# Layer 0's attention in groups of four heads, with mask and sink on VectorE and PE's order fixed in the source

## The chip, the cores and the metric

The kernel runs on one core of a Trainium2 chip. A core has five engines that work side by side, each through its own queue in order: TensorE (PE, with its weight loads shown apart as PEld), VectorE (DVE), ScalarE (ACT), GpSimd (POOL) and SyncE (SP), which here issues transfers. PE writes its results into PSUM, eight banks of 512 f32 columns by 128 partitions; the other data is in SBUF. The metric is the device time of one execution in microseconds (us).

## The reference

A model of several layers of mixed kinds runs on 512 latent positions and 256 context positions of width 1024, all in f32. The change lies in the first layer's mixer, windowed attention with grouped keys and a sink: 16 query heads of 64 columns, 4 key and value heads, each used by 4 query heads. Latent queries are taken in 4 blocks of 128; a block sees itself, its neighbours and all context keys, and within the neighbours only keys at most 128 positions away. Context queries see the context alone.

```python
def softmax_with_sink(s, sink):
    sk = sink.astype(jnp.float32)[None, :, :, None, None]
    m = jnp.maximum(jnp.max(s, axis=-1, keepdims=True), sk)
    e = jnp.exp(s - m)
    return e / (jnp.sum(e, axis=-1, keepdims=True) + jnp.exp(sk - m))
...
        s_lat = jnp.einsum('bqhgd,bkhd->bhgqk', q, k).astype(jnp.float32)
        s_lat = jnp.where(ok, s_lat, NEG_INF)
        s_ctx = jnp.einsum('bqhgd,bkhd->bhgqk', q, k_ctx).astype(jnp.float32)
        p = softmax_with_sink(jnp.concatenate([s_lat, s_ctx], axis=-1), sink_g).astype(v.dtype)
        return (jnp.einsum('bhgqk,bkhd->bqhgd', p[..., :n_loc], v)
                + jnp.einsum('bhgqk,bkhd->bqhgd', p[..., n_loc:], v_ctx))
```

## The kernel before

The program runs the whole model in one launch: layer 0 (this attention and an MLP), layer 1 (a gated scan and an MLP), then a second block (attention with relative positions, a state-space layer, a mixture of experts). Only `layer0_attn` and a helper that it calls are touched.

By the time attention begins, queries `Q` (one tile per head), keys split into a high and a low part (`KH`, `KL`, one each per key head) and values `V` are in SBUF. There are six query blocks `qb` of 128 rows: 0 and 1 are context, 2 to 5 latent. For one query block and one query head (called a head here; there are 6 x 16 = 96) the kernel does the following.

- Scores, in `scores`: matmuls of Q with KH and KL for the latent keys (L618, L619; 384 columns where a block has two neighbours, 256 where it has one), a matmul of the identity with a bf16 mask for each neighbour (L621, L623), matmuls with KH and KL for the 256 context keys (L624, L625), and one of a single column for the sink (L626). So qb 3 and 4 have five key tiles of 128 (640 columns), qb 2 and 5 four, and qb 0 and 1 the two of the context. All of it lands in a two-bank PSUM tile, of which there are two.
- Softmax: DVE takes the negated maximum of a row (L627), ACT the exponential with its sum (L635), from PSUM into `p`, DVE the reciprocal of the sum (L637), and POOL multiplies (L638). The score banks come free when the exponential has read them.
- Values, in `values`, for two key heads (eight heads) at a time and one key tile per step: twice four transposes of p on PE into one bank (L659), copied to SBUF as `pt` by ACT and by DVE (L662), and a pair of value matmuls of 512 columns, one into the upper and one into the lower 64 rows of a bank (L666), which `K.together` keeps side by side. After the last key tile DVE copies the result out (L674).

The loop runs over twelve blocks of eight heads. Between the heads of one block it emits the value steps of the block before. In six places it also runs `K.mod_half`, half of a modulation vector: 32 matmuls of 256 columns with weights loaded into the `raw` buffers (L362), a copy by ACT, and four transposes (L369). After the loop the first two units of the output projection's weights w_o are made ready by `K.unit`: a load into `raw`, a cast on ACT (L221) and a subtraction on DVE (L222). `K.mod_affine` follows, with transposes for a gate (L428). The order of PE's instructions is chosen by the scheduler of the tile framework from the order of emission and from dependences; the other engines' too.

The tiles `p` lie in a pool of ten, and three of a block's in the `wlo` weight buffers; `pt` lies in the `whi` weight buffers and in a tile of its own.

Of the kernel before, what the change touches and what calls it, by code (L numbers as in the profile page):

```python
# [19 lines left out]
P = 128  # L20
# [130 lines left out]
class Kern:  # L151
# [196 lines left out]
    def mod_half(self, pool, l, m, half, tag="rows", raws=("raw", "raw"), own=None):  # L348

        nc = self.nc  # L350
# [14 lines left out]
        rows = pool.tile([P, 4, P], F32, tag=tag, name=self.nm("rows"), bufs=1)  # L365
        nc.scalar.copy(rows, b.rearrange("p (k t) -> p k t", k=4))
        b = self.bank()
        for k in range(4):
            nc.tensor.transpose(b[:, k * P:k * P + P], rows[:, k], self.ident)  # L369
        c0 = 8 * m + 4 * half  # L370
        v = b.rearrange("p (k s r) -> p k r s", k=4, s=4)[:, :, 0:2, :]
        nc.vector.tensor_reduce(self.modT[l][:, c0:c0 + 4, :], v, axis=AX.X, op=ALU.add)  # L372
        bm = self.sm(f"b_mod{l}")[:, c0:c0 + 4]
        nc.vector.tensor_add(self.modT[l][:, c0:c0 + 4, :], self.modT[l][:, c0:c0 + 4, :],
                             bm[:, :, None].to_broadcast([P, 4, 2]))
# [138 lines left out]
def layer0_attn(K):  # L514
# [11 lines left out]
    with ExitStack() as left:  # L526
# [5 lines left out]
        mask = qp.tile([P, 2, P], BF, name="mask")  # L532
        nc.gpsimd.memset(mask, 0.0)
        nc.gpsimd.affine_select(mask[:, 0], mask[:, 0], pattern=[[1, P]], compare_op=ALU.is_ge, fill=NEG,
                                base=0, channel_multiplier=-1)
        nc.gpsimd.affine_select(mask[:, 1], mask[:, 1], pattern=[[-1, P]], compare_op=ALU.is_ge, fill=NEG,
                                base=0, channel_multiplier=1)

        sk = qp.tile([P, 3, 16], BF, name="sk")
        sr = qp.tile([P, 16], F32, name="sr")  # L540
        sink3 = qp.tile([P, 16], BF, name="sink3")
        one3 = qp.tile([P, P], BF, name="one3")
        nc.vector.memset(sink3, 0.0)
        nc.vector.memset(one3, 0.0)
        nc.vector.memset(one3[0:3], 1.0)
        nc.vector.tensor_copy(sk[:, 0], K.sm("sink"))
        nc.vector.tensor_sub(sr, K.sm("sink"), sk[:, 0])
        nc.vector.tensor_copy(sk[:, 1], sr)
        nc.vector.tensor_sub(sr, sr, sk[:, 1])
        nc.vector.tensor_copy(sk[:, 2], sr)  # L550
        for k in range(3):
            nc.scalar.dma_start(sink3[k:k + 1], sk[0:1, k])
# [45 lines left out]
        with K.right("att", 2) as ap:  # L598
            def scores(qb, j):

                lat = qb >= 2
                bl = qb - 2
                w0, w1 = (max(bl - 1, 0), min(bl + 1, 3)) if lat else (0, -1)
                nl = (w1 - w0 + 1) * P
                a0 = 512 - nl
                n = nl + NCTX + 1
                qs = slice(qb * P, qb * P + P)
                nmx, den = K.tiny(4), K.tiny(4)
                pr = []
                if lat and j % 2 == 0:  # L610
                    three = K.w.tile([P, 2048], F32, tag="wlo", name=K.nm("p3"))[:, :1926]
                    three = three.rearrange("p (g n) -> p g n", g=3)
                for g in range(4):
                    h = 4 * j + g
                    S = K.bank2()
                    if lat:
                        ks = slice(NCTX + w0 * P, NCTX + w0 * P + nl)
                        nc.tensor.matmul(S[:, a0:512], Q[h][:, qs], KH[j][:, ks], start=True, stop=False)  # L618
                        nc.tensor.matmul(S[:, a0:512], Q[h][:, qs], KL[j][:, ks], start=False, stop=False)  # L619
                        if w0 < bl:  # L620
                            nc.tensor.matmul(S[:, a0:a0 + P], K.identb, mask[:, 0], start=False, stop=w1 == bl)  # L621
                        if w1 > bl:
                            nc.tensor.matmul(S[:, 512 - P:512], K.identb, mask[:, 1], start=False, stop=True)  # L623
# [1498 lines left out]
```

## Time and profile before

Three runs took 2281.13, 2284.09 and 2289.94 us; the median is 2284.09.

| | us |
|---|---|
| profiled execution, its own time | 2287.39 |
| its span, first to last instruction | 2285.7 |
| PE busy | 2147.8 (94%) |
| PE weight loads busy | 1773.3 (78%) |
| DVE busy | 1391.3 (61%) |
| ACT busy | 963.6 (42%) |
| POOL busy | 321.6 (14%) |
| layer 0's attention, first score matmul to first output projection | 193.4 (142.0 to 335.4) |
| mean granted PE clock of the execution | 0.974 |

The busy times are those of the whole span; engines overlap, so they don't add up to it. The ends of matmuls are modelled and overlap the next ones, so that the distance between the starts of two instructions tells more of what PE spends than the durations do. "Granted clock" is the share of PE's full clock (2.4 GHz) that the chip allowed; 0.5 is its other level (1.2 GHz), and a value between them is a mean over a stretch.

### The profile page before, as it was taken

How to read it: one execution, taken by the hardware profiler on the slowest of the kernel's cores; microseconds unless marked ns; L12 is line 12 of the kernel's file. 1: busy time of each engine (PE TensorE's matmuls, PEld its weight loads, DVE VectorE, ACT ScalarE, POOL GpSimd, SP SyncE). 2: the span in 40 equal slices, each digit the busy share in tenths (PEclk: the TensorE clock that was granted, in tenths of full speed). 3: DMA queues.
4: the chain of work that ended last, by engine and by line, in shares of the span. 5: the costliest groups of instructions: out<-in, count | busy, mean ns of one | idle time of the engine just before them, and what ended most of it. 6: DMA issues, size and time to landing. Idle time of an engine off the chain costs nothing. (4 is left out here: it accounts for less than half of the span.)

```text
span 2285.7 us, 30405 instructions
## 1 busy us (share of the span) xinstructions
PE 2147.8 (94%) x12104; PEld 1773.3 (78%) x12104; DVE 1391.3 (61%) x2343; ACT 963.6 (42%) x1504; POOL 321.6 (14%) x357
## 2 busy tenths in 40 slices
PE   6999989999999999999989999999899997998986
PEld 5876658888888888789977887888799874776864
DVE  4665664899745444641794598555646764547974
ACT  5445555521221221542554532322353453536864
POOL 0025432112000000410000100000220000013422
PEclk9999999999999999999999999999999998998998
DMA  7123021457411211111211224232322435468992
GB/s 289 65 102 112 37 87 44 175 188 254 157 56 56 74 64 66 56 53 56 94 38 38 87 89 151 96 112 81 122 93 93 152 125 125 179 241 289 318 296 73
DMA packets 58064, 279.09 MB, mean 122 GB/s; under 512 B 9345, under 2 KB 13841, under 8 KB 33089
## 3 DMA queue, kind: packets, MB, share of 16 engines
q1 hardware_dynamic: 38048, 219.39, 27.3%
q0 software_dynamic: 18768, 55.04, 7.6%
q10 hardware_dynamic: 1104, 2.70, 0.3%
q8 instruction: 96, 1.57, 0.3%
q14 instruction: 48, 0.39, 0.1%
HBM read 264.54 MB, written 24.08 MB: 126 GB/s over the span
## 5 line engine op out<-in xcount | busy, mean ns | idle before, releaser
L221 ACT CAST whi<-raw 128x2048 fp32r<-128x2048 f32 x106 | 202.4, 1910 | 561.6 <-PE b L252 390.0
L222 DVE TENSOR_TENSOR wlo<-raw,whi 128x2048 fp32r<-128x2048 f32 x106 | 245.1, 2314 | 224.5 <-ACT whi L221 224.3
L250 PE MATMUL b<-hl,whi 128*128 128x512 f32 (+1 forms) x736 | 284.0, 386 | 2.5 <-DVE t L323 1.5
L248 PE MATMUL b<-hl,whi 128*128 128x512 f32 (+1 forms) x736 | 283.0, 385 | 0.8 <-ACT whi L221 0.8
L252 PE MATMUL b<-hl,wlo 128*128 128x512 f32 (+1 forms) x736 | 281.7, 386 | 0.0
L823 DVE TENSOR_TENSOR acc<-acc,b 128x512 f32<-128x512 f32 x280 | 180.8, 682 | 157.0 <-PE b L252 156.7
L248 PE MATMUL b<-whi,hid 128*128 128x512 f32 x640 | 215.5, 395 | 2.6 <-ACT whi L221 1.9
L250 PE MATMUL b<-wlo,hid 128*128 128x512 f32 x640 | 216.7, 394 | 0.0
L252 PE MATMUL b<-whi,hid 128*128 128x512 f32 x640 | 215.0, 395 | 0.0
L250 PEld LDWEIGHTS b<-hl,whi 128*128 128x128 f32 x736 | 139.1, 189 | 30.6 <-issue 3.1
L248 PEld LDWEIGHTS b<-hl,whi 128*128 128x128 f32 x736 | 139.0, 189 | 30.1 <-ACT whi L221 1.3
L252 PEld LDWEIGHTS b<-hl,wlo 128*128 128x128 f32 x736 | 139.3, 189 | 28.3 <-issue 0.2
L1978 DVE TENSOR_TENSOR wlo<-raw,whi 128x2048 fp32r<-128x2048 f32 x57 | 129.9, 2287 | 32.4 <-ACT whi L1978 32.4
L252 PEld LDWEIGHTS b<-whi,hid 128*128 128x128 f32 x640 | 120.3, 188 | 27.9
L248 PEld LDWEIGHTS b<-whi,hid 128*128 128x128 f32 x640 | 119.2, 188 | 29.2 <-ACT whi L221 2.1
L250 PEld LDWEIGHTS b<-wlo,hid 128*128 128x128 f32 x640 | 120.4, 188 | 27.5
L638 POOL TENSOR_TENSOR p<-p,t 128x512 f32<-128x512 f32 (+2 forms) x96 | 91.6, 969 | 177.8 <-DVE modT L372 90.3
L1978 ACT CAST whi<-raw 128x2048 fp32r<-128x2048 f32 x57 | 108.3, 1912 | 10.4 <-PE b L242 10.4
L395 DVE CUSTOM_DVE_ANT_0 junk<-mw,cb 128x1024 bf16<-128x1024 f32 x80 | 97.5, 1219 | 3.2 <-DMA mw<-in_w_modT_dram 2.6
L240 PE MATMUL b<-whi,hl 128*128 128x256 f32 x320 | 91.3, 285 | 2.3 <-ACT qr L1486 2.3
L241 PE MATMUL b<-wlo,hl 128*128 128x256 f32 x320 | 91.5, 286 | 0.0
L242 PE MATMUL b<-whi,hl 128*128 128x256 f32 x320 | 91.1, 285 | 0.0
(617 smaller groups left out, 4736.9 us busy)
## 6 DMA issues: line engine op xcount, KB each, us to landing
raw<-in_w_e_dram SPq DMA_DIRECT2D x57, 1024.0 KB, 7.2
raw<-in_w_mlp_in_dram SPq DMA_DIRECT2D x32, 1024.0 KB, 4.8
raw<-in_w_mlp_out_dram SPq DMA_DIRECT2D x32, 1024.0 KB, 4.8
mw<-in_w_modT_dram POOLq DMA_DIRECT2D x56, 512.0 KB, 4.5
raw<-in_w_mod_dram SPq DMA_DIRECT2D x20, 1024.0 KB, 7.7
raw<-in_w_in_dram SPq DMA_DIRECT2D x16, 1024.0 KB, 4.7
raw<-in_gla_in_dram SPq DMA_DIRECT2D x12, 1024.0 KB, 4.7
raw<-in_w_o_dram SPq DMA_DIRECT2D x8, 1024.0 KB, 4.7
```

Source lines behind the costliest of these rows:

```text
L221: ins = self.nc.scalar.copy(hi, r).ins
L222: ins = ins, (self.nc.gpsimd if pool else self.nc.vector).tensor_sub(lo, r, hi.bitcast(F32)).ins
L240: mm(out, ah, bh, start=start, stop=False)
L241: mm(out, ah, bl, start=False, stop=False)
L242: mm(out, al, bh, start=False, stop=stop)
L248: mm(o, ah, b, start=start, stop=False)
L250: mm(o, ah, b, start=False, stop=False)
L252: mm(o, al, b, start=False, stop=stop)
L395: v.tensor_tensor_reduce(junk, w, cb[b], 1.0, 0.0, ALU.mult, ALU.add, to[:, k, b:b + 1])
L638: nc.gpsimd.tensor_mul(p[:, :n - 1], p[:, :n - 1], den[:, g:g + 1].to_broadcast([P, n - 1]))
L823: nc.vector.tensor_add(a, a, bs[n])
L1978: ins = K.nc.scalar.copy(hi, r).ins, K.nc.vector.tensor_sub(lo, r, hi.bitcast(F32)).ins
```

## The change

Mask and sink leave PE. The mask is now an f32 tile in SBUF, seven key tiles wide, zero except in the two that hold the triangles, so that any block finds its pattern in it as a slice (`added`). One DVE instruction (L623 of the new kernel) adds this slice to the scores from PSUM, multiplies by -1, writes the result to `p` in SBUF, and takes the minimum of the row beginning with the negated sink. POOL copies the negated sink into the column behind the scores (L622), and ACT takes the exponential of `p` in place with scale -1 (L625). Reciprocal and multiply are as before.

Heads are taken in 24 groups of four: two query heads of each of two key heads. A value step is then four transposes (L645), one copy (L648, two of five by DVE), and a pair of value matmuls of 256 columns (L656); `both` is one bank for all groups, a half for each in turn. There are 88 steps with 352 transposes. `p` has 12 buffers and `pt` four.

PE's order is that of the source (`manual_schedule`). After the scores of head x come the steps that `late` lists for x: group v begins its transposes at head 4v + 6, and spreads its key tiles over four heads; the value matmuls run two steps behind the transposes. The modulation halves stand after the scores of heads 14, 29, 44, 59, 74 and 89, with their transposes one head later (`turn`), and the two units of w_o after head 90.

```diff
+    def mod_rows(self, pool, l, m, half, tag="rows", raws=("raw", "raw"), own=None, bufs=1):
...
+        def turn():
...
+        return turn
...
-        mask = qp.tile([P, 2, P], BF, name="mask")
+        mask = qp.tile([P, 7, P], F32, name="mask")
...
+        nsink = qp.tile([P, 16], F32, name="nsink")
+        nc.vector.tensor_scalar(nsink, K.sm("sink"), -1.0, None, op0=ALU.mult)
...
-        with K.right("att", 2) as ap:
+        with K.right("att", 2) as ap, tc.manual_schedule(engines={mybir.EngineType.PE}):
+            added = mask.rearrange("p a b -> p (a b)")
...
+            def head(qb, j, g, p):
...
+                for a, ks in ((al, lat_ and slice(NCTX + lat_[0] * P, NCTX + lat_[-1] * P + P)), (ac, slice(0, NCTX))):
+                    if a is not None:
+                        o = S[:, a:a + ks.stop - ks.start]
+                        nc.tensor.matmul(o, Q[h][:, qs], KH[j][:, ks], start=True, stop=False)
+                        nc.tensor.matmul(o, Q[h][:, qs], KL[j][:, ks], start=False, stop=True)
+                nmx, den = K.tiny(1), K.tiny(1)
+                ns = nsink[:, h:h + 1]
+                nc.gpsimd.tensor_copy(p[:, n:n + 1], ns)
+                nc.vector.tensor_tensor_reduce(p[:, :n], S[:, a0:a0 + n], added[:, z:z + n], -1.0, ns,
+                                               ALU.add, ALU.min, nmx)
+                nc.scalar.activation(p[:, :n + 1], p[:, :n + 1], AF.Exp, bias=nmx, scale=-1.0, accum_out=den)
+                nc.vector.reciprocal(den, den)
+                nc.gpsimd.tensor_mul(p[:, :n], p[:, :n], den.to_broadcast([P, n]))
...
-                    if w0 < bl:
-                            nc.tensor.matmul(S[:, a0:a0 + P], K.identb, mask[:, 0], start=False, stop=w1 == bl)
-                    nc.tensor.matmul(S[:, 512 + NCTX:513 + NCTX], one3, sink3[:, h:h + 1], start=True, stop=True)
-                    nc.vector.reduce_max(nmx[:, g:g + 1], S[:, a0:a0 + n], axis=AX.X, negate=True)
...
+            for qb, jj in ((2, 0), (3, 0), (0, 0), (4, 0), (5, 0), (1, 0), (2, 1), (3, 1), (0, 1), (4, 1), (1, 1), (5, 1)):
+                for gp in range(2):
+                    groups.append((qb, 2 * jj, 2 * gp, [], window(qb)[5]))
+                    heads += [(groups[-1], i, g) for i in range(2) for g in range(2)]
+            both = K.bank()
...
+                    late.setdefault(4 * v + 6 + c * 4 // len(kts), []).append((v, c))
...
+            def turned(v, c):
+                T = K.bank()
+                for x, p in enumerate(groups[v][3]):
+                    nc.tensor.transpose(T[:, x * P:x * P + P], p[:, c * P:c * P + P], K.ident)
+                w = ap.tile([P, 512], F32, tag="pt", name=K.nm("pt"), bufs=4)
+                n_t[0] += 1
+                (nc.vector.tensor_copy if n_t[0] % 5 in (1, 3) else nc.scalar.copy)(w, T)
+                held.append((v, c, w))
...
+                    nc.tensor.matmul(O[i * 64:i * 64 + 64], V[:, kts[c], (j + i) * 64:(j + i) * 64 + 64],
+                                     w[:, i * 256:i * 256 + 256], start=c == 0, stop=c == len(kts) - 1,
...
+            for x in range(len(heads) + 12):
...
+                        p = ap.tile([P, 642], F32, tag="p", name=K.nm("p"), bufs=12)
...
+                    head(group[0], group[1] + i, group[2] + g, ps)
+                if turn:
+                    turn()
+                    turn = None
+                elif mods and x % 15 == 14:
+                    turn = K.mod_rows(ap, *mods.pop(0), tag="pt", bufs=4)
+                for item in late.get(x, ()):
+                    turned(*item)
+                    if len(held) > 2:
+                        value()
+                if x == len(heads) - 6:
+                    w_o = [K.unit(A["w_o0"][u]) for u in range(2)]
```

On PE, one head against five key tiles in the kernel before: its scores in the middle of the attention (`b` is the score bank, `Q_414` the query head).

```order
L618 MATMUL b_236_1744<-KH_430,Q_414 128x384
L619 MATMUL b_236_1744<-KL_434,Q_414 128x384
L621 LDWEIGHTS identb
L621 MATMUL b_236_1744<-mask,identb 128x128
L623 LDWEIGHTS identb
L623 MATMUL b_236_1744<-mask,identb 128x128
L624 MATMUL b_236_1744<-KH_430,Q_414 128x256
L625 MATMUL b_236_1744<-KL_434,Q_414 128x256
L626 LDWEIGHTS one_450
L626 MATMUL b_236_1744<-sink_449,one_450 128x1
```

In the new kernel the same kind of head, with the value step that stands behind it (`p_...` are the four heads of a group, `b_1252` is the bank `both`).

```order
L618 MATMUL b_206_1461<-KH_430,Q_416 128x384
L619 MATMUL b_206_1461<-KL_434,Q_416 128x384
L618 MATMUL b_206_1461<-KH_430,Q_416 128x256
L619 MATMUL b_206_1461<-KL_434,Q_416 128x256
L645 MATMUL b_1473<-ident,p_1305 128x128
L645 MATMUL b_1473<-ident,p_1318 128x128
L645 MATMUL b_1473<-ident,p_1331 128x128
L645 MATMUL b_1473<-ident,p_1351 128x128
L656 MATMUL b_1252<-pt_1433,v 64x256 x2
```

The masks and the sink with their weight loads are gone, and a step of four transposes and one pair of value matmuls follows each such head.

On POOL, where context heads give way to latent ones for the first time, in the kernel before: multiplies only (128x256 are context heads, 128x640 latent ones).

```order
L638 TENSOR_TENSOR p_1729<-p_1729,t_1691 128x256 [waits DVE_49,PE_49,Pool_49]
L638 TENSOR_TENSOR p_1729<-p_1729,t_1691 128x256 [waits DVE_49]
L638 TENSOR_TENSOR p_235_1743<-p_235_1743,t_1742 128x640 [waits DVE_49] x3
L638 TENSOR_TENSOR p_1850<-p_1850,t_1742 128x640 [waits DVE_49,Pool_49]
L638 TENSOR_TENSOR p_1865<-p_1865,t_1855 128x640 [waits DVE_49]
L638 TENSOR_TENSOR p_1878<-p_1878,t_1855 128x640 [waits DVE_49,Pool_49]
L638 TENSOR_TENSOR p_1891<-p_1891,t_1855 128x640 [waits DVE_49,Pool_49]
```

The same place in the new kernel: `p_1745`, `p_1768`, `p_1781` and `p_1803` are heads 24 to 27, and `p_1980` and `p_2012` heads 34 and 35.

```order
L627 TENSOR_TENSOR p_1745<-p_1745,t_1752 128x640 [waits DVE_49]
L627 TENSOR_TENSOR p_1768<-p_1768,t_1775 128x640 [waits DVE_49]
L622 COPY p_1980<-nsink 128x1 [waits PE_49,Pool_49]
L622 COPY p_2012<-nsink 128x1 [waits PE_49,Pool_49]
L627 TENSOR_TENSOR p_1781<-p_1781,t_1788 128x640 [waits DVE_49]
L627 TENSOR_TENSOR p_1803<-p_1803,t_1810 128x640 [waits DVE_49]
L627 TENSOR_TENSOR p_1816<-p_1816,t_1823 128x640 [waits DVE_49]
```

Copies for later heads now stand between the multiplies. Such a copy waits for PE, namely for the last transposes of the head whose buffer it takes (a context head of group 5, transposed at heads 26 and 28), and the multiplies of heads 26 and 27 stand behind it.

On ACT, near the end of the attention, in the kernel before: w_o's first cast (L221) among the exponentials of the last twelve heads.

```order
L635 ACTIVATE p_3044,t_2984<-b_471_3036,t_2983 128x513 [waits DVE_49]
L221 CAST whi_3213<-raw_3211 128x2048 [waits DMAHW7_49,PE_49,Activation_49]
L635 ACTIVATE p_3055,t_3049<-b_475_3050,t_3048 128x257 [waits DVE_49,Pool_49]
L635 ACTIVATE p_3055,t_3049<-b_481_3075,t_3048 128x257 [waits DVE_49]
L635 ACTIVATE p_3088,t_3049<-b_482_3083,t_3048 128x257 [waits DVE_49]
L635 ACTIVATE p_3088,t_3049<-b_486_3106,t_3048 128x257 [waits DVE_49]
L662 COPY pt_3060<-b_3092 128x512 [waits PE_49]
```

In the new kernel the first cast stands ahead of the exponential of head 91 and the second ahead of that of head 94 (`p_3275` is head 91, `p_3324` head 94).

```order
L648 COPY pt_3259<-b_3254 128x512 [waits PE_49]
L221 CAST whi_3265<-raw_3263 128x2048 [waits DMAHW4_49]
L625 ACTIVATE p_3275,t_3282<-p_3275,t_3281 128x513 [waits DVE_49,Activation_49]
L648 COPY pt_3306<-b_3301 128x512 [waits PE_49,Activation_49]
L625 ACTIVATE p_3288,t_3295<-p_3288,t_3294 128x513 [waits DVE_49,Pool_49]
L625 ACTIVATE p_3311,t_3318<-p_3311,t_3317 128x513 [waits DVE_49,Pool_49]
L221 CAST whi_3271<-raw_3269 128x2048 [waits DMAHW5_49]
L625 ACTIVATE p_3324,t_3331<-p_3324,t_3330 128x513 [waits DVE_49,Activation_49]
```

The casts wait for their loads, and what stands behind them on ACT waits too. Here the first cast is five heads from the end, where it was eight before. The loads go into the `raw` buffers, which the modulation half after head 89 is the last to use.

## Rows read from the trace of the kernel before

**Rows 1.** attention by stretches: length, PE, PEld, DVE, ACT, POOL busy, clock, DMA.

```profile
142.00:163.00 21.00, 16.89 (x115) 12.40 (x113) 14.71 (x33) 12.57 (x29) 10.03 (x10) 0.84 0.40 151
163.00:292.00 129.00, 124.22 (x948) 79.67 (x947) 81.81 (x192) 69.87 (x173) 65.76 (x69) 1.00 0.22 83
292.00:335.40 43.40, 35.77 (x225) 23.56 (x223) 24.48 (x52) 21.37 (x49) 15.82 (x19) 0.92 0.15 50
142.00:335.40 193.40, 176.88 (x1283) 115.64 (x1281) 121.00 (x276) 103.82 (x250) 91.62 (x96) 0.96 0.23 83
```

**Rows 2.** PE's waits in 142 to 335.4: total us, times, longest.

```profile
PE b L659 <- POOL p L638: 5.4, 6, 1.4
PE b L666 <- DVE pt L662: 4.9, 6, 1.5
```

**Rows 3.** PE's timeline at 215: start, us, engine, line, operation; five-tile head, value step.

```profile
215.20 0.63 PE L659 MATMUL b<-ident,p 128*128 128x128 f32 x4
215.59 0.42 PE L618 MATMUL b<-KH,Q 128*128 128x384 f32 x1
...
216.03 0.23 PE L621 MATMUL b<-mask,identb 128*128 128x128 bf16 x1
...
216.12 0.36 PE L624 MATMUL b<-KH,Q 128*128 128x256 f32 x1
...
216.45 0.18 PE L626 MATMUL b<-sink,one 128*128 128x1 bf16 x1
216.49 0.63 PE L659 MATMUL b<-ident,p 128*128 128x128 f32 x4
217.05 1.08 PE L666 MATMUL b<-pt,v 128*64 128x512 f32 x4
218.06 1.09 PE L659 MATMUL b<-ident,p 128*128 128x128 f32 x8
```

**Rows 4.** the same view at 148: a four-tile head, first and next.

```profile
148.11 0.36 PE L618 MATMUL b<-KH,Q 128*128 128x256 f32 x1
...
148.83 0.31 PE L659 MATMUL b<-ident,p 128*128 128x128 f32 x1
```

**Rows 5.** the same view at 226: a modulation half.

```profile
226.21 1.93 PE L362 MATMUL b<-raw,csil 128*32 128x256 f32 x32
```

**Rows 6.** the same view in the second block: a value pair 256 wide.

```profile
1876.60 0.65 PE L1593 MATMUL b<-pt,v 128*64 128x256 f32 x4
1877.18 0.50 PE L1563 MATMUL b<-KH,Q 128*128 128x512 f32 x1
```

**Rows 7.** DVE, 142 to 335.4, by line: count, busy us, mean ns, idle.

```profile
L627 DVE TENSOR_REDUCE t<-b 128x1 f32<-128x641 f32 x32 | 26.3, 823 | 9.6 <-PE b L626 8.4
L637 DVE RECIPROCAL t<-t 128x1 f32<-128x1 f32 x96 | 14.9, 159 | 22.9 <-ACT p L635 21.9
```

**Rows 8.** the same view of the second block, 1785 to 1900.

```profile
L1566 DVE CUSTOM_DVE_ANT_0 s<-b,tb 128x512 f32<-128x512 f32 x8 | 5.5, 690 | 12.0 <-PE b L1564 8.0 <-ACT whi L221 4.0
...
L1566 DVE DVE_READ_ACCUMULATOR2_ANT t<- 128x1 f32 x32 | 2.7, 83 | 0.1
```

**Rows 9.** ACT by line in 142 to 335.4.

```profile
L635 ACT ACTIVATE p<-b,t 128x641 f32<-128x641 f32 x32 | 25.5, 798 | 24.8 <-DVE t L627 24.6
```

**Rows 10.** POOL by line in 142 to 335.4.

```profile
L638 POOL TENSOR_TENSOR p<-p,t 128x640 f32<-128x640 f32 x32 | 39.7, 1254 | 30.2 <-DVE t L637 24.9 <-DVE modT L374 5.3
L638 POOL TENSOR_TENSOR p<-p,t 128x512 f32<-128x512 f32 x32 | 32.8, 1041 | 113.5 <-DVE modT L372 90.3 <-DVE t L637 20.2 <-DVE modT L374 2.9
L638 POOL TENSOR_TENSOR p<-p,t 128x256 f32<-128x256 f32 x32 | 19.1, 613 | 34.0 <-DVE t L637 29.2 <-DVE modT L374 4.8
```

**Rows 11.** w_o's cast and subtraction, ACT and DVE by line.

```profile
L221 ACT CAST whi<-raw 128x2048 fp32r<-128x2048 f32 x2 | 3.8, 1894 | 0.5 <-ACT p L635 0.5
...
L222 DVE TENSOR_TENSOR wlo<-raw,whi 128x2048 fp32r<-128x2048 f32 x2 | 4.6, 2288 | 0.7 <-ACT whi L221 0.7
```

**Rows 12.** DMA issues of the page: KB, us to landing.

```profile
raw<-in_w_o_dram SPq DMA_DIRECT2D x8, 1024.0 KB, 4.7
```

More of the change, by code (lines that the diff above doesn't have):

```diff
@@ L348, in mod_half @@
     def mod_half(self, pool, l, m, half, tag="rows", raws=("raw", "raw"), own=None):
+        self.mod_rows(pool, l, m, half, tag, raws, own)()
+    def mod_rows(self, pool, l, m, half, tag="rows", raws=("raw", "raw"), own=None, bufs=1):
         nc = self.nc
@@ L364, in mod_half @@
                                      skip_group_check=True)
-        rows = pool.tile([P, 4, P], F32, tag=tag, name=self.nm("rows"), bufs=1)
+        rows = pool.tile([P, 4, P], F32, tag=tag, name=self.nm("rows"), bufs=bufs)
         nc.scalar.copy(rows, b.rearrange("p (k t) -> p k t", k=4))
[L367 to L375, printed above, removed]
+        def turn():
+            b = self.bank()
+            for k in range(4):
+                nc.tensor.transpose(b[:, k * P:k * P + P], rows[:, k], self.ident)
+            c0 = 8 * m + 4 * half
+            v = b.rearrange("p (k s r) -> p k r s", k=4, s=4)[:, :, 0:2, :]
+            nc.vector.tensor_reduce(self.modT[l][:, c0:c0 + 4, :], v, axis=AX.X, op=ALU.add)
+            bm = self.sm(f"b_mod{l}")[:, c0:c0 + 4]
+            nc.vector.tensor_add(self.modT[l][:, c0:c0 + 4, :], self.modT[l][:, c0:c0 + 4, :],
+                                 bm[:, :, None].to_broadcast([P, 4, 2]))
+        return turn
     def mod_dots(self, gp, wp):
@@ L531, in layer0_attn @@
         V = qp.tile([P, 6, 256], F32, name="v")
-        mask = qp.tile([P, 2, P], BF, name="mask")
+        mask = qp.tile([P, 7, P], F32, name="mask")
         nc.gpsimd.memset(mask, 0.0)
-        nc.gpsimd.affine_select(mask[:, 0], mask[:, 0], pattern=[[1, P]], compare_op=ALU.is_ge, fill=NEG,
+        nc.gpsimd.affine_select(mask[:, 2], mask[:, 2], pattern=[[1, P]], compare_op=ALU.is_ge, fill=NEG,
                                 base=0, channel_multiplier=-1)
-        nc.gpsimd.affine_select(mask[:, 1], mask[:, 1], pattern=[[-1, P]], compare_op=ALU.is_ge, fill=NEG,
+        nc.gpsimd.affine_select(mask[:, 4], mask[:, 4], pattern=[[-1, P]], compare_op=ALU.is_ge, fill=NEG,
                                 base=0, channel_multiplier=1)
[L539 to L552, printed above, removed]
+        nsink = qp.tile([P, 16], F32, name="nsink")
+        nc.vector.tensor_scalar(nsink, K.sm("sink"), -1.0, None, op0=ALU.mult)
         with st:
```

120 lines of the change are left out of this document (35 added, 85 removed).

## The prediction

> **What bounds the kernel now.** I read the table of busy engines first: PE is busy 94% of the span and no other engine passes 61%, so a change to one stage pays by what it does to PE there. The change touches layer 0's attention, 193.4 us from its first score matmul at 142.0 to the first output projection at 335.4, 8.5% of the span; the table by stretches [rows 1] shows what kind of stage it is. PE is busy 16.89 of 21.0 us at the start, 124.22 of 129.0 in the middle and 35.77 of 43.4 at the end: it is idle 4.1, 4.8 and 7.6 us, and in the first and the last stretch the granted clock averages 0.84 and 0.92 instead of 1.00, which costs another 3.4 (21.0 x 0.16) and 3.5 us (43.4 x 0.08). DVE (121.0), ACT (103.8) and POOL (91.6) are far from 193.4. The waits name POOL's multiply before transposes (5.4 us) and DVE's copies before value matmuls (4.9 us) [rows 2].
>
> Matmul ends overlap in the records, so I take what PE spends from the distance between starts [rows 3 to 5]. A head against five key tiles takes 0.90 us (215.59 to 216.49); four tiles 0.72 (148.11 to 148.83); a context head is the part of the first from L624 on, 0.37. There are 32 heads of each kind: 63.7 us. Four transposes take 0.39 before scores (215.20 to 215.59) and 0.56 before value matmuls (216.49 to 217.05); a value pair of 512 columns takes 1.01 (217.05 to 218.06). A value step is two times four transposes and one pair, 0.39 + 0.56 + 1.01 = 1.96, and 44 steps are 86.2 us. A modulation half is 1.93 [rows 5] and four transposes more (0.39): six are 13.9. The gate's 32 transposes are eight times 0.39, 3.1. Sum 166.9, so about 26.5 us of the stage are no work of PE; idle and clock above explain 23.4 of them.
>
> **PE's work after.** The mask matmuls go (0.09 of the five-tile head, 216.03 to 216.12; I take half of that in a four-tile one, which has one mask instead of two), and so does the sink matmul (0.04, 216.45 to 216.49). That is 32 x 0.13 + 32 x 0.085 + 32 x 0.04 = 8.2 us; the matmul that then stands behind another large one instead of a small one may start up to 0.03 sooner, which in 64 heads is 1.9, so -8.2 to -10.1, and I take -9.
>
> The value step is halved: with two heads of each of two key heads instead of four, a pair is 256 columns wide and there are 88 of them. In the second block the same shape stands in the trace: four such records start at 1876.60 and the next work at 1877.18, 0.58 us [rows 6]; as the 512-wide pair has four records too, this is one pair. A step is then 0.56 + 0.58 = 1.14, and 88 are 100.3 us, +14.1. From below: if the second block's transition did not repeat, half of 1.01 would give 0.51 and 94.2, +8.0.
>
> The row shows that four transposes cost 0.17 more ahead of a value pair than ahead of scores (0.56 against 0.39 [rows 3]), and that half the width costs more than half the time (0.58 against 0.51). The Trainium skill, TensorEngine Tiling (Array Packing), Tiling Modes, says of going from one tiling to another that "Mode switching requires drain": the value matmuls use half of the array's columns (128*64 in the rows), the transposes all (128*128), and the change doubles these transitions. By that rule the pairs cost what the rows say, +14.1; without it 88 x (0.39 + 0.51) = 79.2 would stand against 44 x (0.39 + 0.39 + 1.01) = 78.8, nothing. The trace agrees with the rule.
>
> So PE's own work goes from 166.9 to 166.9 - 9 + 14.1 = 172.0 us, +5 (bounds -2 and +6). The change pays only if it takes away waits, of which there are 26.5.
>
> **The other engines.** DVE's maximum over 641 columns takes 823 ns [rows 7]. The operation that replaces it, sum with a mask, scale and minimum from PSUM and SBUF, stands in the second block at 690 ns for 512 columns [rows 8]. Between these two I take the same cost per column as the maximum, about 0.83 for 640, plus a read of the accumulator, 0.08 [rows 8]. 96 x 0.08 is 8 us more on DVE, to some 129 of about 190: hidden under PE, except where heads come without value steps between them (below). The exponential now reads SBUF; its bounds are 0 and the 798 ns of today [rows 9], and as ACT has half the stage free it is nothing either way. What does change is when the score banks come free: behind DVE's operation instead of behind ACT's exponential, 0.8 us sooner with two banks, which takes the waits of score matmuls for ACT out of the order. POOL gets 96 copies of one column. No copy of that width on POOL stands in this stage; I bound one by 0 and the 613 ns of the smallest multiply [rows 10], take 0.1 (it is one column against 256), and get 10 us on an engine that is busy 92 of 193. They matter by their place, not their length. A copy goes into a buffer that the transposes of three groups back must have left, and POOL works in order, so the multiplies behind it wait as well. In most places such a copy waits for a transpose five heads ahead of the first transposes that need the multiplies behind it. In three places (where a context group is followed by latent ones: heads 26, 50 and 75) it is two heads, with one or two multiplies of 1.04 to 1.25 us to do in some 2 us of PE work. That is about 1 us each.
>
> **The waits after.** *Start.* PE now has only scores until head 6, then the transposes of group 0, which need four heads through DVE, ACT and POOL (0.69 + at most 0.80 + 0.16 + 1.04 for the last of them alone), behind the last rotary work on DVE as before. I keep today's 4.1 + 3.4 = 7.5 and add 1.5 for the fixed order, which lets nothing else go ahead: 9 (6 to 11). *Middle.* Between a group's last scores and its first transposes lie three heads and about as many value steps, 3 x 0.77 + 3 x 1.14 = 5.7 us for the five-tile kind, against a chain of 0.83 + 0.80 + 0.16 + 1.25 = 3.0 us and the queues. That is covered. Where context heads give way to latent ones, six latent heads have only three context steps beside them: 6 x 0.77 + 3 x 1.14 = 8.0 us of PE against 6 x (0.83 + 0.08 + 0.16) = 6.4 on DVE with three to four copies more, close to a tie. With the three POOL places I take 5 us for all 24 groups (0 to 10), against 4.8 idle and some waits for weight loads before. *End.* The order puts the last modulation half at head 89 and the two w_o units at 90; their raw loads can only start when that half has left the buffers. Then: landing 4.7 [rows 12], ACT's cast 1.89, DVE's subtraction 2.29 [rows 11], and behind these on both queues the exponential and reciprocal of head 91 (0.16) and its multiply (1.04): 10.1 us, in which PE has five four-tile heads (3.2), two context steps (2.3), four transposes (0.4) and little else, some 6.5. That is a stall of 3.5 us. I add 1.7 for the cast of the output, which the first projection waits for in either kernel, and for the clock: 5.2, where today there are 7.6 + 3.5 = 11.1.
>
> Together 9 + 5 + 5.2 = 19.2, so 172.0 + 19.2 = 191.2 against 193.4. As PE's bounds (-2 to +6) lie mostly under its +5, I take 190.5: a gain of 3 us. The profiled execution took 2287.4 us (span 2285.7), so 2284.4 by its own time; it lies 3.3 above the median of the runs, 2284.1, so on the median's scale it is 2281. All of this is far inside 0.5% (11.4 us), about what a measurement of this kernel can tell from no change.
>
> **Rivals.**
> *Every wait covered.* Waits fall to the start's 9 and 1.3 at the end, and PE's work to its lower bounds (scores -10.1, steps +8.0, 164.8): 175.1, -18.3; with +14.1 in the steps 181.2, -12.2. Time 2266 to 2272. For it: the queue between transposes and value matmuls is two steps deep now, and 4.9 us of waits for copies [rows 2] go; against it: the w_o chain is in the order itself.
> *POOL decides each group.* In a fixed order nothing can go past a transpose that waits. If the multiplies, with copies ahead of them that wait for PE, come one instruction late in each of 24 groups, PE waits 8 x (1.25 + 1.04 + 0.61) = 23 us [rows 10] instead of 5: 190.5 + 18 = 208.5, +15, time 2299, slower. It decides from the point where the three heads of lag (5.7 us) are less than chain and queues; the 5.4 us of waits on this multiply today speak for it, the lag against it.
> *The waits stay.* All 26.5 us of today come back in other places (start, POOL, w_o) on top of PE's +5: 198.5, time 2289.
> *The narrower pairs cost less than the second block shows.* Steps +8.0 instead of +14.1, the rest as forecast: 2275; that is inside the forecast's own range.
>
> **How the numbers follow.** Forecast 0.45 (2274 to 2286 with its bounds), every wait covered 0.27, the waits stay 0.15, POOL decides 0.13. Faster by over 0.5% (under 2272.7) takes most of the second, and a little of the first: 0.28. Slower by over 0.5% (over 2295.5) takes most of the fourth and a part of the third: 0.16. The rest, 0.56, is no change. The range of 2264 to 2296 holds the forecast, most of the first rival and the third, and leaves the slow one out.
>
> **What would show it.** In the profile after: no mask or sink matmuls; 88 pairs 256 wide with 1.1 us from the first transpose of a step to the next scores (right), or 0.9 (the narrower pairs are cheap). PE's waits for the multiply at most some 5 us in the middle, at the starts of groups 6, 12 and 18; if they stand at every group, POOL decides. One wait of 3 to 4 us at the end, before the transposes of head 91's group, behind the casts of w_o. A granted clock under 1.00 in the first 15 us and at that wait. The forecast is wrong if the stage is under 183 or over 202 us long, or if the time moves outside this stage: nothing else is changed there.

## The result and the profile after

The new kernel takes 2270.4 us (median of 5 runs, 2268.2 to 2274.9) against 2284.1; the ratio is 0.9936, 95% interval 0.9916 to 0.9956. The profiled execution took 2268.2 us, its span 2266.2. The attention runs from 140.3 to 324.9, 184.5 us instead of 193.4. A second profile of the same kernel, taken later, gives 185.0; this one pair is all that tells how far stage lengths of single profiles can be relied on. One run of a kernel below, two_pairs, took 2396.4 us at a mean granted clock of 0.84 where the others have 0.97, and is left out of that kernel's time and ratio.

The table by stretches answers to [rows 1], with the same columns; the last row is the whole stage.

```profile
140.30:161.30 21.00, 16.03 (x89) 12.30 (x87) 15.58 (x42) 13.99 (x29) 12.95 (x26) 0.84 0.14 51
161.30:285.00 123.70, 121.60 (x928) 80.10 (x928) 81.55 (x269) 76.58 (x184) 76.92 (x142) 1.00 0.23 86
285.00:324.90 39.90, 35.20 (x261) 22.87 (x261) 23.44 (x67) 20.98 (x45) 14.20 (x25) 0.96 0.29 108
140.30:324.90 184.60, 172.83 (x1274) 115.27 (x1272) 120.56 (x376) 111.55 (x258) 104.08 (x192) 0.97 0.23 87
```

PE is idle 5.0, 2.1 and 4.7 us in the three parts. What PE spends is read from the distance between starts again, as in [rows 3, 4]: the timeline of a five-tile head with a value step, of a four-tile head, and of a context head.

```profile
157.80 0.44 PE L618 MATMUL b<-KH,Q 128*128 128x384 f32 x1
...
158.26 0.28 PE L618 MATMUL b<-KH,Q 128*128 128x256 f32 x1
158.37 0.28 PE L619 MATMUL b<-KL,Q 128*128 128x256 f32 x1
158.49 0.60 PE L645 MATMUL b<-ident,p 128*128 128x128 f32 x4
159.02 0.65 PE L656 MATMUL b<-pt,v 128*64 128x256 f32 x4
159.60 0.44 PE L618 MATMUL b<-KH,Q 128*128 128x384 f32 x1
...
200.54 0.38 PE L618 MATMUL b<-KH,Q 128*128 128x256 f32 x1
...
201.12 0.60 PE L645 MATMUL b<-ident,p 128*128 128x128 f32 x4
...
217.90 0.39 PE L618 MATMUL b<-KH,Q 128*128 128x256 f32 x1
...
218.25 0.60 PE L645 MATMUL b<-ident,p 128*128 128x128 f32 x4
```

The heads take 0.69, 0.58 and 0.35 us, the step 0.53 + 0.58 = 1.11. So PE's own work is 32 x (0.69 + 0.58 + 0.35) + 88 x 1.11 + 13.9 + 3.1 = 166.5 us, where it was 166.9; the other 18.0 of 184.5 are waits and clock, where it was 26.5.

Within a five-tile head the context matmul of KL starts 0.11 us after that of KH (158.26 to 158.37). Before, behind the masks, it was 0.20: KH's stands at 216.12 in [rows 3], and KL's is this one.

```profile
216.32 0.28 PE L625 MATMUL b<-KL,Q 128*128 128x256 f32 x1
```

PE's waits in the stage answer to [rows 2].

```profile
PE b L645 <- POOL p L627: 7.2, 5, 3.4
PE b L618 <- DVE t L623: 2.4, 4, 1.0
PE b L248 <- ACT oh L699: 1.3, 1, 1.3
PE b L618 <- DVE r L560: 0.6, 1, 0.6
PE b L656 <- ACT p L625: 0.3, 1, 0.3
```

No wait is put down to the copies `pt` any more (4.9 before). The waits for the multiply stand at the start (2.0 in two places), near the end (3.4), and in between only where context heads give way to latent ones, as the timeline shows: at group 12 and, small, at group 18.

```profile
235.32 0.33 PE L645 MATMUL b<-ident,p 128*128 128x128 f32 x1 [1.35 <-POOL p L627]
...
278.75 0.33 PE L645 MATMUL b<-ident,p 128*128 128x128 f32 x1 [0.45 <-POOL p L627]
...
307.93 0.33 PE L645 MATMUL b<-ident,p 128*128 128x128 f32 x1 [3.38 <-POOL p L627]
```

The last of them, before the transposes of group 22, stands behind w_o's chain on ACT, DVE and POOL: cast, subtraction, multiply. The cast itself waited 0.77 us for its load.

```profile
302.45 1.91 ACT L221 CAST whi<-raw 128x2048 fp32r<-128x2048 f32 x1 [0.77 <-DMA raw<-in_w_o_dram]
...
304.39 2.29 DVE L222 TENSOR_TENSOR wlo<-raw,whi 128x2048 fp32r<-128x2048 f32 x1
...
306.84 3.04 POOL L627 TENSOR_TENSOR p<-p,t 128x512 f32<-128x512 f32 x3 [4.32 <-DVE t L626]
```

At groups 12 and 18 POOL itself had been idle before the multiply that PE waited for, 0.84 and 0.98 us, until DVE's reciprocal was done:

```profile
234.23 4.04 POOL L627 TENSOR_TENSOR p<-p,t 128x512 f32<-128x512 f32 x4 [0.84 <-DVE t L626]
...
277.45 3.67 POOL L627 TENSOR_TENSOR p<-p,t 128x640 f32<-128x640 f32 x3 [0.98 <-DVE t L626]
```

**Outside the stage.** Behind it the output projection runs at full clock, where before its first 9.6 us had a mean of 0.82. The two rows are the stretches of the kernel before and of the new one.

```profile
335.40:345.00 9.60, 9.59 (x35) 7.56 (x36) 6.85 (x4) 6.34 (x5) 0.00 (x0) 0.82 0.99 377
```

```profile
324.87:334.00 9.13, 9.07 (x38) 7.16 (x39) 6.83 (x4) 6.32 (x5) 0.00 (x0) 1.00 0.98 380
```

The 30th matmul after the first comes 7.4 instead of 8.6 us behind it: 1.2 us. That the first score matmul came 1.6 us sooner can't be put down to the change: in the fourteen profiles it lies between 139.9 and 142.8, in no order of what the kernels contain (141.3 in the second profile of the new one). Stage and projection are 10 of the 13.7 us; the remaining 3 to 4 lie within the interval and were not located.

### The profile page after: what moved, and what is told of

The parts are those of the page before. It is cut to its first block, busy times and chain, and to the rows that moved or that the text cites. A ratio compares the mean times of both kernels' runs of the same rounds, so it can differ in the third digit from the quotient of the medians.

```text
span 2266.2 us, 30706 instructions
## 1 busy us (share of the span) xinstructions
PE 2138.9 (94%) x12088; PEld 1769.3 (78%) x12088; DVE 1390.6 (61%) x2436; ACT 971.2 (43%) x1512; POOL 334.8 (15%) x453
## 5 line engine op out<-in xcount | busy, mean ns | idle before, releaser
L221 ACT CAST whi<-raw 128x2048 fp32r<-128x2048 f32 x106 | 202.4, 1909 | 559.3 <-PE b L252 389.1
L1970 ACT CAST whi<-raw 128x2048 fp32r<-128x2048 f32 x57 | 108.4, 1912 | 10.7 <-PE b L242 10.6
```

What stands on the lines that cost most here:

```text
L221: ins = self.nc.scalar.copy(hi, r).ins
L1970: ins = K.nc.scalar.copy(hi, r).ins, K.nc.vector.tensor_sub(lo, r, hi.bitcast(F32)).ins
```

## Experiments

The stage is that of one profile each; times are medians, with the ratio to the kernel before run beside them. "Idle" is the stage less PE's busy time, "clock" is the stage times what its mean granted clock lacks of 1, as in the prediction, and "rest" is what is left: an estimate of PE's own work.

| kernel | stage, us | idle | clock | rest | blocks of value matmuls | time, us | ratio (95%) |
|---|---|---|---|---|---|---|---|
| before | 193.4 | 16.5 | 6.8 | 170.1 | 43 | 2284.1 to 2286.7 | |
| masks_only | 169.1 | 10.2 | 3.4 | 155.6 | 43 | 2257.6 | 0.987 (0.985 to 0.989) |
| masks_twice | 178.4 | 8.1 | 0.0 | 170.3 | 44 | 2268.1 | 0.992 (0.990 to 0.994) |
| before_nomask | 186.5 | 20.4 | 10.2 | 155.9 | 44 | 2275.2 | 0.994 (0.992 to 0.997) |
| hold_bank | 190.7 | 22.0 | 10.3 | 158.4 | 44 | 2279.1 | 0.997 (0.995 to 0.999) |
| pe_masks | 198.0 | 8.4 | 5.1 | 184.4 | 86 | 2295.8 | 1.004 (1.002 to 1.005) |
| free_order | 176.3 | 8.6 | 0.0 | 167.7 | 72 | 2266.9 | 0.991 (0.989 to 0.993) |
| new kernel (again) | 184.5 (185.0) | 11.8 (12.2) | 5.1 (5.1) | 167.6 (167.7) | 86 | 2270.4 (2272.7) | 0.994 (0.992 to 0.996) |
| mods_early | 182.9 | 10.2 | 5.1 | 167.6 | 86 | 2275.8 | 0.994 (0.992 to 0.996) |
| mods_early2 | 180.7 | 11.1 | 1.7 | 167.9 | 86 | 2267.1 | 0.991 (0.987 to 0.994) |
| two_pairs | 170.6 | 10.2 | 3.4 | 157.0 | 44 | 2262.0 | 0.990 (0.988 to 0.993) |
| lag2 | 236.9 | 43.4 | 23.9 | 169.6 | 86 | 2324.3 | 1.017 (1.014 to 1.019) |
| masks_two_steps | 164.4 | 9.6 | 3.4 | 151.3 | 25 | 2259.2 | 0.987 (0.985 to 0.990) |

A block is a run of value matmuls with nothing else of PE between them, as the trace has them in order. The rests agree within 0.4 us for before and masks_twice, for masks_only and before_nomask, and for the new kernel and the two with early halves, which have the same instructions on PE; what differs within such a group is idle time and clock. hold_bank, with the instructions of masks_only, is 2.9 us above it, so the rest isn't quite free of the order. The times move by some microseconds outside the stage as well: mods_early has a shorter stage than the new kernel and no better ratio. So the argument goes by the stage.

**masks_only: the masks without groups and order.**

```diff
-                    nc.vector.reduce_max(nmx[:, g:g + 1], S[:, a0:a0 + n], axis=AX.X, negate=True)
+                    nc.gpsimd.tensor_copy(p[:, n:n + 1], ns)
+                    nc.vector.tensor_tensor_reduce(p[:, :n], S[:, a0:a0 + n], added[:, z:z + n], -1.0, ns,
+                                                   ALU.add, ALU.min, nmx[:, g:g + 1])
```

> The kernel before with one part of the change: mask, sink and maximum in one DVE instruction, POOL copying the negated sink, exponential in place; groups of eight heads, value pairs of 512 columns and the scheduler's order of PE as before. Theory W (the gain is waits that the fixed order takes away, while PE's own work stays about the same because the halved steps give back what the masks save): PE's work falls by 8 to 10 us, but its waits for POOL's multiply and for copies stay or grow, as less work lies between them; the stage of 193.4 us gets 2 to 7 us shorter. Rival M (the gain is the masks alone): the stage falls by the full 9 to 11 us, as far as with the whole change or further, since the wide pairs stay. Both expect the first score matmul 1.6 us sooner, since the sink's split leaves DVE.

The stage fell by 24.3 us: theory W is wrong, and rival M falls short as well, as it counts on 9 to 11. One third of the change does nearly three times what the whole does in the stage, and by the ratios (0.987 against 0.994) twice as much in the time. Of the 24.3 us, 14.5 are in the rest, so the masks' price of 8 to 10 on PE was too low; 6.4 are idle time and 3.4 clock.

**pe_masks: groups and order without the masks.** In the new kernel `head` has the old masks, sink column, maximum and exponential.

> The new kernel with masks and sink put back on PE (bf16 masks, the sink's column, maximum and exponential from PSUM, as before), groups of four and the fixed order kept. Theory W: 8 to 10 us of PE's work come back and the score banks are held until the exponential has read them; the stage is 184.6 + 9 to 13 = 194 to 198 us, as long as before or a little longer, and the first score matmul is 1.6 us later than in the new kernel. Rival M: the same 9 us, but no more, about 193 to 194. Under a third reading, that the order alone carries the gain, the stage stays near 186.

198.0, at the upper end of W's range and beyond M's: 13.4 us over the new kernel, more than the masks had been priced at on PE. Its rest is 16.8 us above the new kernel's and its idle time 3.3 below: with the order fixed, score banks held until the exponential cost no more waits than the new kernel has. Against the kernel before, groups and order by themselves cost 4.5 us: 14.3 more in the rest, 8.1 less idle time and 1.7 less by the clock.

**free_order: masks and groups without the order.**

```diff
-        with K.right("att", 2) as ap, tc.manual_schedule(engines={mybir.EngineType.PE}):
+        with K.right("att", 2) as ap:
```

> The new kernel without the fixed order: the scheduler places PE's instructions, all else as in the new kernel. Theory W: waits come back, as transposes are placed as soon as the scheduler expects their data, 5 to 10 us on the stage of 184.6; they show as waits of transposes for POOL and of value matmuls for copies in the middle, where the new kernel has 1.8 us of them. Rival M: the order is worth nothing, the stage stays within 2 us of 184.6.

The other way: 8.2 us shorter, and PE's waits for POOL are 0.8 us and for copies 0.7 in the whole stage. The rest is that of the new kernel, so the order changes nothing in PE's own work by this measure: the new kernel has 3.1 us more idle time, in the middle (2.1 against 0.9) and at the end (4.7 against 3.0), and 5.1 us by the clock, where free_order is at 1.00 throughout. Why its clock held, with as much idle time at the start (4.8 against 5.0), is open.

```profile
142.39:163.00 20.61, 15.81 (x105) 11.69 (x103) 17.28 (x47) 14.89 (x32) 14.07 (x27) 1.00 0.17 52
163.00:280.00 117.00, 116.12 (x894) 77.08 (x892) 76.80 (x257) 70.19 (x175) 72.97 (x139) 1.00 0.25 91
280.00:318.70 38.70, 35.75 (x278) 23.50 (x278) 25.16 (x73) 23.41 (x53) 19.08 (x27) 1.00 0.32 110
```

With the steps in a row, before 193.4, masks 169.1, groups 176.3, order 184.5, the change is -24.3, +7.2 and +8.2.

**masks_twice and before_nomask: what the 24.3 us are.** The first adds PE's mask and sink matmuls to masks_only again; the second takes them out of the kernel before.

> The kernel masks_only (mask, sink and maximum on DVE, the rest as before; stage 169.1 us) with PE's 96 mask matmuls and 96 sink matmuls put back beside it, so that the mask is added twice and the sink's column is read by nobody. It separates what PE saves from what the earlier release of the score banks (behind DVE's operation instead of ACT's exponential) saves. Theory P: the 24.3 us of masks_only are mostly PE's work, by the new spacing of heads 0.23, 0.15 and 0.08 us in 32 heads each, some 15 us; so the stage is 169.1 + 13 to 16 = 182 to 185. Rival B: the bank's release carries it, the mask matmuls lie in waits; the stage stays at 170 to 176.

> The kernel before without the mask and sink matmuls, and with nothing in their place (the result leaves out mask and sink); maximum and exponential still read the score bank, which the exponential releases. The other half of the same question. Theory P: the stage of 193.4 us falls by the same 13 to 16 us, to 177 to 180, and the 8 to 9 us left up to masks_only's 169.1 are the earlier release. Rival B: it falls by under 8 us.

Theory P fails for the stage: the matmuls alone are worth 9.3 us (169.1 to 178.4) or 6.9 (193.4 to 186.5). For PE's own work it was right, 14.7 or 14.2 us in the rest, but without the matmuls 5.4 or 7.3 us come back as idle time and clock. The larger part, 15.0 from 193.4 to 178.4, comes with every one of them still on PE: 8.4 us of idle time and 6.8 by the clock, which is at 1.00 in masks_twice. Without them on PE the same step is 17.4 us, 186.5 to 169.1.

```profile
140.63:319.03 178.40, 170.26 (x1284) 112.09 (x1282) 124.43 (x372) 106.99 (x250) 102.99 (x189) 1.00 0.25 90
```

**hold_bank: the release of the score banks.**

```diff
+                    nc.scalar.copy(K.tiny(1), S[:, a0:a0 + 1])
                     nc.vector.reciprocal(den[:, g:g + 1], den[:, g:g + 1])
```

> The kernel masks_only (stage 169.1 us), with one addition: behind the exponential ACT copies one column of the scores from the bank to a tile that nobody reads, so that the bank is released by ACT after the exponential, as in the kernel before. PE's instructions are those of masks_only; ACT gets 96 copies of about 0.2 us. If the earlier release is what carried the 15 us between the kernel before and masks_twice (193.4 to 178.4), the stage goes back up by 10 to 15 us, to 179 to 184, with waits of score matmuls for ACT and of transposes for POOL. If those 15 us had another reason (the exponential from SBUF, POOL's copies, another order of the scheduler), the stage stays within 3 us of 169.1.

190.7, beyond the range on the expected side: 21.6 us come back, 11.8 of them idle time and 6.9 clock, with the same instructions on PE. The scheduler orders them differently, and the 21.6 hold what comes of that too. PE's waits of masks_only, and then of hold_bank, over the stage:

```profile
PE b L617 <- DVE t L628: 4.0, 7, 1.3
...
PE b L661 <- DVE pt L657: 1.1, 2, 0.9
PE b L654 <- POOL p L633: 1.0, 2, 0.6
```

```profile
PE b L617 <- ACT t L632: 9.6, 17, 1.4
PE b L662 <- DVE pt L658: 6.1, 8, 1.3
PE b L655 <- POOL p L634: 4.6, 7, 1.3
```

Held until ACT has read them, the two banks stop the scores (9.6), and scores that come late make multiplies and copies late (4.6 and 6.1). The kernel before showed the same three, the last two in [rows 2] and the first in this line of the same answer:

```profile
PE b L618 <- ACT p L635: 4.0, 5, 1.4
```

ACT's 96 extra copies lengthen the hold a little beyond that of the kernel before, so 21.6 is an upper figure. The low clock returns too, in the stage (0.95 against 0.98) and in the first 9.6 us of the projection (0.83):

```profile
140.48:331.19 190.71, 168.71 (x1091) 106.87 (x1089) 123.68 (x372) 111.95 (x346) 103.76 (x189) 0.95 0.22 84
331.19:340.79 9.60, 9.60 (x35) 7.76 (x36) 6.84 (x4) 6.33 (x5) 0.00 (x0) 0.83 0.94 345
```

**two_pairs: fewer changes between transposes and value matmuls, in the fixed order.**

```diff
-                    if len(held) > 2:
+                    if len(held) > 3:
+                        value()
                         value()
```

> The new kernel with its fixed order, in which value pairs are issued two at a time (two steps of transposes, then two pairs of value matmuls side by side), so that there are about 44 changes between transposes and value matmuls instead of 88; the number of instructions is the same. Theory S (changing between the full array and half of it costs PE time): a step and its pair take 0.53 + 0.58 now, and two of them 0.39 + 0.53 + 1.02 if only every second one pays for the change, 0.28 us less; 41 to 44 times that is 11 to 12 us: stage 184.5 - 10 to 12 = 172 to 175, below the 176.3 of the free order, whose scheduler put some pairs together by itself. Rival: the narrow pair costs what it costs, and the stage stays within 3 us of 184.5.

170.6, 14.0 less with the same instructions. The rest falls by 10.7 us, 0.25 for each of 42 blocks, where 11.8 were expected at 0.28; idle time falls by 1.6 and the clock's part by 1.7. Before group 22 the wait of 3.4 is gone, and group 23 waits 1.1 (0.47 + 0.67). So taking turns 86 times has its price in the fixed order. It isn't what sets the new kernel behind free_order, though: that has 72 blocks and the same rest, and why its 14 blocks fewer don't show there is open. The timeline shows two pairs in 1.01 us, 189.28 to 190.29, where each alone takes 0.58.

```profile
188.75 0.60 PE L645 MATMUL b<-ident,p 128*128 128x128 f32 x4
189.28 1.08 PE L656 MATMUL b<-pt,v 128*64 128x256 f32 x8
190.29 0.44 PE L618 MATMUL b<-KH,Q 128*128 128x384 f32 x1
```

**mods_early and mods_early2: the wait near the end.**

```diff
-                elif mods and x % 15 == 14:
+                elif mods and x % 15 == 3:
```

In mods_early w_o's units moved to head 80 as well.

> The new kernel with the modulation halves after heads 3, 18, 33, 48, 63 and 78 instead of 14 to 89, and w_o's two units after head 80 instead of 90. If the 3.4 us for which PE waits near the end come from w_o's loads, which start when the last half has left the raw buffers, they go, and with them the low clock behind them: 4 to 5 us; the half after head 3 fills 1 to 2 us of the wait at the start. Stage 184.6 - 5 to 7 = 178 to 180. If the wait at the end is that of POOL's multiplies for other reasons (the copies of the sink, the reciprocals), it stays and the stage is 183 to 185.

> The new kernel with the modulation halves after heads 3, 18, 33, 48, 63 and 78, and w_o's units left after head 90. In mods_early the units had moved along with the last half, and ACT's cast waited 2.5 us for the load there. Now twelve heads lie between. If the load after the last half is the cause, the wait of 3.4 us near the end goes and none comes in its place: with the low clock that followed, stage 182.9 - 3.5 to 5 = 178 to 179.5. If the casts themselves, 1.9 us each on ACT ahead of the exponentials, make the wait, 1 to 2 us of it stay and the stage is 180.5 to 182.

182.9 in mods_early is just under the second range. The cast follows the last half as closely as before and waits for the load in its new place; ACT's timeline has it:

```profile
283.65 1.90 ACT L221 CAST whi<-raw 128x2048 fp32r<-128x2048 f32 x1 [2.46 <-DMA raw<-in_w_o_dram]
```

mods_early2 was to put twelve heads between, and doesn't: only PE's order is fixed, and on ACT the scheduler left the cast behind the last half, where it waits for its load as in mods_early. PE's order is the same in the two kernels, instruction by instruction.

```profile
283.38 1.90 ACT L221 CAST whi<-raw 128x2048 fp32r<-128x2048 f32 x1 [2.40 <-DMA raw<-in_w_o_dram]
```

So neither run takes the wait away, and the two readings of mods_early2 stay undecided; both move it. Of the 3.38 us before group 22 0.67 are left, and 2.42 stand before group 19, behind the cast's new place. So the wait goes with w_o's chain of load, cast and subtraction. Beside it, the halves had been cover where context heads give way to latent ones: group 6, which had one before it, now waits 1.59 us, group 12 waits as before (1.36), and group 18, which has one now, no longer does.

```profile
194.57 0.33 PE L645 MATMUL b<-ident,p 128*128 128x128 f32 x1 [1.59 <-POOL p L627]
...
237.33 0.33 PE L645 MATMUL b<-ident,p 128*128 128x128 f32 x1 [1.36 <-POOL p L627]
...
290.07 0.33 PE L645 MATMUL b<-ident,p 128*128 128x128 f32 x1 [2.42 <-POOL p L627]
...
308.13 0.33 PE L645 MATMUL b<-ident,p 128*128 128x128 f32 x1 [0.67 <-POOL p L627]
```

Of the 3.8 us by which this stage is shorter than the new kernel's, 3.4 are clock (0.99 against 0.97) and 0.7 idle time.

**lag2: a shorter lag.** `4 * v + 4` for `4 * v + 6`.

> The new kernel with the first transposes of a group one head after its last scores instead of three (4v + 4 for 4v + 6), the order fixed as before. The lag then covers one head and one or two value steps, 1.7 to 3 us, against the chain of 3.0 us over DVE, ACT and POOL with its queues. The slow rival of the prediction, POOL's multiply deciding at every group in a fixed order, then comes true: waits of 0.6 to 2 us before the first transposes of most of the 24 groups, stage 184.5 + 15 to 35 = 200 to 220. If the lag of three heads was not needed, the stage stays within 5 us of 184.5.

The mechanism holds, and its size was put too low: 52.4 us. The slow rival of the prediction comes true: the waits for the multiply are 39.7 us in 38 places, and the mean clock of the stage falls to 0.90, which makes the rest longer.

```profile
PE b L645 <- POOL p L627: 39.7, 38, 5.3
```

```profile
139.89:376.78 236.89, 193.46 (x1273) 122.82 (x1271) 121.62 (x376) 112.86 (x258) 106.68 (x192) 0.90 0.18 68
```

**masks_two_steps: the masks, and the value pairs of two steps together.** As in two_pairs, but 512 columns wide and with the scheduler's order.

> The kernel masks_only with the value pairs of two steps emitted behind the transposes of both, as in two_pairs, but 512 wide and with PE's order left to the scheduler. If all 43 blocks of value matmuls became 24, at 0.27 us each that is 5 us off 169.1, 164 to 165; as the scheduler places some of them apart, 165 to 168. If the copies of the second step come too late for the longer block, waits of value matmuls for copies take it back and the stage is 169 to 172.

164.4, at the lower end, with 4.3 us less in the rest than masks_only. Its time, 2259.2, can't be told from masks_only's 2257.6; both are under the new kernel's by some 0.6%.

**after_again.**

> The new kernel once more, on the chip of these runs: its time beside that of the other kernels, and a second profile of it. The stage lengths compared here come from single profiles; if they can be relied on, this one is 184.5 within 1 us. The first score matmul came at 140.3 in its first profile and between 140.2 and 142.8 in the others; if that spread is one between executions, not one of the change, it comes anywhere in it.

185.0 and 141.3, as said above.

## Why the prediction came out as it did

The time lies in the stated range but not at the likeliest case: 10.6 us under it, and under 2272.7, to which 0.28 was given. It is at the number of the rival "every wait covered", and not by its mechanism, since waits and clock did not fall to 10 but to 18.0, as forecast (19.2). The stage is at the number of another rival, the cheaper pairs (190.5 - 6.1 = 184.4), and that is luck for the most part: the steps cost 11.5 us more, not its 8.0, and the other half of the difference comes from the heads.

- *PE's own work* was put at +5 and came out at -0.4. The heads saved 11.8 instead of 9: at 0.69, 0.58 and 0.35 they lie under the bound of the masks alone. The price of a mask was taken up to the next start (0.09 for two), but the matmul behind the masks took 0.09 longer as well, 0.20 instead of 0.11. The steps cost 11.5 instead of 14.1; four transposes ahead of a value pair take 0.53 behind a large score matmul, not the 0.56 that they took behind the sink's small one. This is the mis-sized step of the sum, over 5 of the 6 us by which the stage was missed. The rests of the table, which need no choice of places, put it at -2.4 (170.1 to 167.6): -14.5 for the masks (masks_only) instead of -9, and +12.1 for the groups (from there to free_order) instead of +14.1. So the masks' price is the term furthest off.
- *The waits after*: start 9 forecast; 5.0 idle and 3.4 of clock, 8.4, measured. Middle 5; 2.1 idle. End 5.2, 3.5 of it for w_o's chain; 4.7 idle and 1.6 of clock, with 3.38 before the transposes of head 91's group. The three places where POOL's copies were to press are the right ones: two show, and mods_early2 shows why group 6 doesn't, as a modulation half stands there. The reason isn't the copies: POOL had been idle before the multiplies in question and waited for DVE's reciprocal.
- *What the change is worth in parts* was misread, which the sum hid. The release of the score banks 0.8 us sooner was given no number beyond the named waits of score matmuls for ACT, and is worth 15 us in the scheduler's order (masks_twice), nearly all of it idle time and clock, as late scores also made the waits put down to POOL and DVE in [rows 2]. The fixed order, taken to cost 1.5 us, costs 8.2, of which 5.1 are clock.
- *Doubled transitions* were priced at 14.1 with the width, and nothing without. By two_pairs a change and its return cost 0.25 to 0.28 us. The Trainium skill's rule on switching tilings (TensorEngine Tiling (Array Packing), Tiling Modes) agrees with that, and a step of the sum could have gone on from it: the cost belongs to the alternation, which the order could have avoided.
- *"Nothing else is changed there"* left out the projection behind the stage, 1.2 us by the clock.

## What to carry to other kernels

Ask of a PSUM bank when it comes free before asking what its producer costs: with two banks, an operation that moves the scores to SBUF as it takes the maximum was worth more than the matmuls it replaced (15.0 us against 9.3). That holds for the scheduler's order; with PE's order fixed, pe_masks held its banks until the exponential as well and had no more idle time than the new kernel (8.4 us against 11.8). A wait put down to an engine late in a chain may be made by a bank at its beginning; the test is an extra reader that holds the bank. Where PE changes between shapes that use different parts of the array, group what has the same shape, and time one part of a bundled change alone: here the first third gained 24 us and the other two gave back 15. And take a stage apart into idle time, clock and the rest before giving a reason: what the fixed order cost lay in the first two, not in PE's work.

## What was not expected of the hardware

Two value pairs of 256 columns in a row take 1.01 us, the same as one pair of 512, while one by itself takes 0.58 with the return. The clock at the end of one stage can cost the next one too: in three of the fourteen profiles (before, before_nomask, hold_bank) the first matmuls of the projection run at a mean granted clock of 0.82 to 0.83 and the 30th after the first comes 1.2 us later than in the other eleven. What decides it there was not tested: lag2, with the most waits of all, is among the eleven.
